# Expert gate and up projections: high and low rows side by side in one 512-column matmul

## The chip, the cores and the metric

The kernel runs on one core of one Trainium2 chip. The metric is the device time of one execution in microseconds (us). TensorE (PE in the profile) multiplies, and its weight loads have a row of their own (PEld). VectorE (DVE), ScalarE (ACT) and GpSimd (POOL) work element by element; SyncE's queue (SP) and POOL's issue transfers. Each engine takes its instructions in the order in which they stand in its queue.

## The reference, cut to what matters

One layer of a diffusion backbone: a token mixer, then a mixture of 16 experts, with float32 throughout. The change lies in the experts. Each expert picks 256 of 2048 tokens, and computes with D = 1024 and EXPERT_FF = 1024

```python
xe = jax.vmap(lambda hb, ib: hb[ib])(h, idx)
hid = jax.nn.silu(jnp.einsum("becd,edf->becf", xe, w_gate)) * jnp.einsum("becd,edf->becf", xe, w_up)
ye = jnp.einsum("becf,efd->becd", hid, w_down) * gate[..., None].astype(h.dtype)
```

and the rows of `ye` are added back at the picked tokens. A final RMSNorm closes the layer.

## The kernel before, in words

Everything up to the routing scores (the mixer) takes the first 1321 us and is not touched. `moe` (from line 1206) then runs the 16 experts one after another.

Float32 products are made of three matmuls of a rounded type: each operand is split into a high part and the low remainder, and `mm3` (line 193) issues high x high (line 194), high x low (195) and low x high (196) into the same PSUM sum. Weights are split by `load_w` (line 167): per half of a 512-column chunk one transfer into `raw` (two buffers), one ACT copy that rounds to `wh` (line 183), one DVE subtraction that gives `wl` (line 184). An expert has six chunks: two of gate, two of up, two of down. Three chunk buffers (two in the pool `wr`, one in `wx`) go round, so a chunk's `wh` can be written only when PE is done with an older chunk.

`expert_in` (line 1364) finds the tokens of the next expert on DVE and PE (`route`, tiles `oh`, `c`, `idx`), gathers their rows with two indirect transfers on POOL's queue (`xg`, line 1368), transposes them on PE (`xt`, line 1376) and splits them into `xS[0]` (high, ACT, line 1378) and `xS[1]` (low, DVE, line 1379), one buffer each. It is called in the middle of the expert before.

`expert` (line 1382) goes over two halves `i` and four blocks `f` of 128 hidden columns. For each it fills one PSUM tile `pg` (name `gu`, 128 x 2 x 256, a whole bank; three buffers): gate in the first 256 columns, up in the other 256, each from 8 steps `k` of `mm3`, 24 matmuls with 256 moving columns. Then ACT takes the SiLU of the gate half out of PSUM (`sgl`, line 1396), DVE multiplies by the up half out of PSUM (1397), ACT rounds the product to `hS[0]` (1399) and DVE makes the remainder `hS[1]` (1400). The down projection (`down`, PSUM name `dn`, two banks) uses 512 moving columns. Results leave by an indirect transfer (1453). In experts 13 and 14 the final norm of all tokens runs beside the matmuls; the last three experts write their rows directly.

The order of each queue is made when the program is built: a scheduler lays the instructions out by its own estimate of their times (`schedule_with_timeline_sim`, line 1567), single matmuls included, so work of neighbouring steps is interleaved. On the chip the queues then run strictly in that order.

Of the kernel before, what the change touches and what calls it, by code (L numbers as in the profile page):

```python
# [7 lines left out]
F32 = mybir.dt.float32  # L8
F32R = mybir.dt.float32r
# [3 lines left out]
AF = mybir.ActivationFunctionType  # L13
OP = mybir.AluOpType
AX = mybir.AxisListType
# [3 lines left out]
P = 128  # L19
D = 1024  # L20
KT = 8
# [1184 lines left out]
def moe(tc, ctx, env):  # L1206
    nc = tc.nc
# [5 lines left out]
    with ExitStack() as pd:  # L1213
# [5 lines left out]
        ps_a = pd.enter_context(tc.tile_pool(name="psaD", bufs=3, space=PS))  # L1219
# [5 lines left out]
        wk = tk.enter_context(tc.tile_pool(name="wkT", bufs=1))  # L1225
# [106 lines left out]
        wk = pd.enter_context(tc.tile_pool(name="wkD", bufs=1))  # L1332

        def route(e):
            oh = ohp.tile([P, 2, 8, 256], BF, name="oh", bufs=1)
            for s in range(2):
                for g in range(8):
                    nc.vector.tensor_scalar(oh[:, s, g, :], siob, SL[:, s, e, g:g + 1], None, op0=OP.is_equal)
            rp = ps_c.tile([P, 2, 256], F32, name="c")
            for hf in range(2):  # L1340
                for i in range(16):
                    s, g = divmod(i, 8)
                    nc.tensor.matmul(rp[:, hf, 0:5], oh[:, s, g, hf * P:(hf + 1) * P], vals[:, s, e, g, :],
                                     start=(i == 0), stop=(i == 15))
            idx = rt.tile([P, 2], I32, name="idx", bufs=2)
            with nc.allow_low_precision(reason="token numbers are whole"):
                nc.vector.tensor_reduce(idx, rp[:, :, 0:2], axis=AX.X, op=OP.add)
            rs = rt.tile([P, 2, 5], F32, name="rs", bufs=2)
            nc.vector.tensor_copy(rs, rp[:, :, 0:5])
            gate = rt.tile([P, 2], F32, name="gate", bufs=2)  # L1350
            nc.vector.tensor_tensor(gate, rs[:, :, 2], rs[:, :, 3], op=OP.add)
            nc.vector.tensor_tensor(gate, gate, rs[:, :, 4], op=OP.add)
            return idx, gate
# [3 lines left out]
        def next_w(src):  # L1357
            if pre:
                return pre.pop(0)
            pool = wx if nchunk[0] % 3 == 2 else wr  # L1360
            nchunk[0] += 1
            return load_w(raw_p, pool, src)

        def expert_in(e):
            idx, gate = route(e)
            xg = wk.tile([P, 2, D], F32, name="xg", bufs=1)
            for hf in range(2):
                last[1] = nc.gpsimd.indirect_dma_start(out=xg[:, hf, :], out_offset=None, in_=f_rows,
                                                       in_offset=bass.IndirectOffsetOnAxis(ap=idx[:, hf:hf + 1], axis=0))
            xS = [wk.tile([P, KT, 256], F32R, name=f"xS{s}", bufs=1) for s in range(2)]  # L1370
            for kk in range(4):
                ps = ps_t.tile([P, 2, 256], F32, name="xt")
                for k2 in range(2):
                    for hf in range(2):
                        k = 2 * kk + k2
                        nc.tensor.transpose(ps[:, k2, hf * P:(hf + 1) * P], xg[:, hf, k * P:(k + 1) * P], ident)  # L1376
                ks = slice(2 * kk, 2 * kk + 2)
                nc.scalar.activation(xS[0][:, ks, :], ps, AF.Copy)
                last[0] = nc.vector.tensor_tensor(xS[1][:, ks, :], ps, xS[0][:, ks, :].bitcast(F32), op=OP.subtract)
            return idx, gate, xS  # L1380

        def expert(e, st, mid=None):
            idx, gate, xS = st
            nx = None
            hS = [wk.tile([P, KT, 256], F32R, name=f"hS{s}", bufs=1) for s in range(2)]
            for i in range(2):
                gw = next_w(w_gate[0, e, :, i * 512:(i + 1) * 512])
                uw = next_w(w_up[0, e, :, i * 512:(i + 1) * 512])
                for f in range(4):
                    fs = slice(f * P, (f + 1) * P)  # L1390
                    pg = ps_a.tile([P, 2, 256], F32, name="gu")
                    for j, w in enumerate((gw, uw)):
                        for k in range(KT):
                            mm3(pg[:, j, :], w[0][:, k, fs], w[1][:, k, fs], xS[0][:, k, :], xS[1][:, k, :], k, KT)
                    sg_ = wk.tile([P, 256], F32, name="sgl", bufs=2)
                    nc.scalar.activation(sg_, pg[:, 0, :], AF.Silu)
                    nc.vector.tensor_tensor(sg_, sg_, pg[:, 1, :], op=OP.mult)  # L1397
                    ff = 4 * i + f
                    nc.scalar.activation(hS[0][:, ff, :], sg_, AF.Copy)  # L1399
                    nc.vector.tensor_tensor(hS[1][:, ff, :], sg_, hS[0][:, ff, :].bitcast(F32), op=OP.subtract)  # L1400
                if mid is not None and i == 0:
                    nx = mid()
# [79 lines left out]

        last = [None, None]
        st = expert_in(0)
        with tc.issue_after(last[1].ins):
            pre.append(load_w(raw_p, wx, w_gate[0, 0, :, 512:1024], cast=C2))
        for e in range(NE):
            nx = mid = None
            if e + 1 < NE:
                if e in MIDE:  # L1490
                    mid = lambda: expert_in(e + 1)
                else:
                    nx = expert_in(e + 1)
            for t in FTS.get(e, ()):
                final_tile(t)
            st = expert(e, st, mid) or nx
# [98 lines left out]
```

## Time and profile before

| | us |
|---|---|
| three runs, median (lowest to highest) | 2491.65 (2488.15 to 2493.32) |
| the profiled execution, its own time | 2490.03 |
| its span, first to last instruction | 2488.2 |
| busy: PE / PEld / DVE / ACT / POOL | 2358.8 / 2156.8 / 1584.1 / 1115.6 / 533.7 |
| stretch of the experts' matmuls | 1321 to 2479 |

How to read it: busy time is a sum over the whole span, and the rows that matter are those of the stretch of the experts. Matmuls are pipelined, so the mean duration of one (some 286 ns) is longer than the distance from the start of one to the start of the next; the distance is what a stream of them costs. "Idle before" is the time for which the engine stood still just before the instruction, with the instruction that released it behind the arrow. The notation 128x2 <- 128x4 is partitions by elements of output and input.

### The profile page before, as it was taken

The page shows a single profiled execution, that of the slowest core. Times are in us where ns is not written, and L with a number is a line of the kernel's source. Part 1 is how long each engine was busy: PE and PEld are TensorE (multiplying, and loading weights), DVE is VectorE, ACT ScalarE, POOL GpSimd, SP SyncE. Part 2 cuts the span into 40 slices and gives each one's busy share as a digit, 9 for nine tenths or more (in the row PEclk, how much of TensorE's full clock was granted, in tenths as well). Part 3 has the DMA queues.
Part 4 walks back from the last instruction along what each step waited for, and adds up shares of the span by engine and source line. Part 5 has one row for each costly group of instructions (what it writes and reads, how often), then busy time and mean ns, then how long its engine had stood idle before and what let it go on. Part 6 is the DMA issues. An engine that isn't in the chain of part 4 may idle for free.

```text
span 2488.2 us, 43191 instructions
## 1 busy us (share of the span) xinstructions
PE 2358.8 (95%) x16841; PEld 2156.8 (87%) x16841; DVE 1584.1 (64%) x3339; ACT 1115.6 (45%) x2004; POOL 533.7 (21%) x451
## 2 busy tenths in 40 slices
PE   7999999999997989999949999999999999999998
PEld 4999999887776888888838899999999999998897
DVE  7588765458778646576774556555565565556675
ACT  4554555567633443333332444444444444444453
POOL 2321222211114553232250101101111011011111
PEclk9999999999998999999978999999999999999999
DMA  8676655489956897655563667666676666668884
GB/s 267 199 229 208 208 172 164 134 269 325 284 142 192 253 278 233 197 187 175 174 189 111 203 187 223 199 205 204 203 220 200 207 219 199 210 203 261 305 301 166
DMA packets 473056, 528.97 MB, mean 213 GB/s; under 512 B 104500, under 2 KB 392061, under 8 KB 470803
## 3 DMA queue, kind: packets, MB, share of 16 engines
q1 hardware_dynamic: 455298, 465.63, 58.6%
q0 software_dynamic: 17120, 59.77, 8.3%
q8 instruction: 133, 2.18, 0.4%
q10 hardware_dynamic: 432, 0.79, 0.1%
q14 instruction: 73, 0.59, 0.1%
HBM read 400.45 MB, written 125.67 MB: 211 GB/s over the span
## 4 chain that ended last, share of the span: by engine, by line
PE 45%; DMA 9%; DVE 3%; issue 3%; ACT 1%; POOL 1%; SPq 0%; POOLq 0%; DVEq 0%; ACTq 0%
PE gu L196 7%; PE gu L194 7%; PE gu L195 7%; PE dn L194 4%; PE dn L195 4%; PE dn L196 4%; DMA xg<-f_rows,idx 4%; PE mx L194 2%; PE mx L196 2%; PE mx L195 2%; DMA raw<-in_w_gate_dram 1%; ACT wh L183 1%; PE xt L1376 1%; DVE wl L184 1%; DMA raw<-in_w_up_dram 1%
## 5 line engine op out<-in xcount | busy, mean ns | idle before, releaser
L184 DVE TENSOR_TENSOR wl<-raw,wh 128x2048 fp32r<-128x2048 f32 (+1 forms) x214 | 450.4, 2116 | 294.2 <-ACT wh L183 291.4
L194 PE MATMUL gu<-xS,wh 128*128 128x256 f32 x2048 | 582.8, 286 | 6.6 <-ACT wh L183 4.7
L196 PE MATMUL gu<-xS,wl 128*128 128x256 f32 x2048 | 580.4, 286 | 4.2 <-DVE wl L184 4.2
L195 PE MATMUL gu<-xS,wh 128*128 128x256 f32 x2048 | 582.0, 285 | 0.0
L183 ACT ACTIVATE wh<-raw 128x2048 fp32r<-128x2048 f32 (+1 forms) x218 | 381.8, 1771 | 356.0 <-DMA raw<-in_w_gate_dram 142.7
L194 PEld LDWEIGHTS gu<-xS,wh 128*128 128x128 f32 x2048 | 395.9, 194 | 8.7 <-ACT wh L183 5.3
L196 PEld LDWEIGHTS gu<-xS,wl 128*128 128x128 f32 x2048 | 394.2, 193 | 6.0 <-DVE wl L184 5.0
L195 PEld LDWEIGHTS gu<-xS,wh 128*128 128x128 f32 x2048 | 396.1, 193 | 1.1
L194 PE MATMUL pj<-aS,wh 128*128 128x258 f32 x832 | 238.7, 290 | 3.1 <-DVE y L460 2.7
L195 PE MATMUL pj<-aS,wh 128*128 128x258 f32 x832 | 239.0, 288 | 0.2 <-DVE aS L358 0.2
L196 PE MATMUL pj<-aS,wl 128*128 128x258 f32 x832 | 238.3, 288 | 0.9 <-DVE wl L184 0.9
L1453 POOL DMA_INDIRECT h_rows<-ye,idx x26 | 67.4, 2591 | 659.8 <-DVE ye L1416 565.7
L194 PE MATMUL dn<-wh,hS 128*128 128x512 f32 (+1 forms) x520 | 202.7, 390 | 0.0
L195 PE MATMUL dn<-wl,hS 128*128 128x512 f32 (+1 forms) x520 | 201.2, 387 | 0.0
L196 PE MATMUL dn<-wh,hS 128*128 128x512 f32 (+1 forms) x520 | 200.3, 386 | 0.0
L194 PEld LDWEIGHTS pj<-aS,wh 128*128 128x128 f32 x832 | 157.7, 191 | 4.7 <-issue 2.4
L195 PEld LDWEIGHTS pj<-aS,wh 128*128 128x128 f32 x832 | 159.2, 191 | 0.6 <-DVE aS L358 0.4
L196 PEld LDWEIGHTS pj<-aS,wl 128*128 128x128 f32 x832 | 158.5, 191 | 1.3 <-DVE wl L184 1.1
L194 PE MATMUL uv<-wh,ast 128*128 128x512 f32 x384 | 153.1, 399 | 0.0
L196 PE MATMUL uv<-wh,ast 128*128 128x512 f32 x384 | 150.2, 391 | 0.0
L195 PE MATMUL uv<-wl,ast 128*128 128x512 f32 x384 | 149.8, 390 | 0.0
L1399 ACT ACTIVATE hS<-sgl 128x256 fp32r<-128x256 f32 x128 | 53.1, 415 | 181.9 <-DVE sgl L1397 181.6
(480 smaller groups left out, 4562.7 us busy)
## 6 DMA issues: line engine op xcount, KB each, us to landing
raw<-in_w_gate_dram SPq DMA_DIRECT2D x64, 1024.0 KB
raw<-in_w_up_dram SPq DMA_DIRECT2D x64, 1024.0 KB
raw<-in_w_down_dram SPq DMA_DIRECT2D x64, 1024.0 KB
kv<-kv SPq DMA_DIRECT2D x140, 256.0 KB
raw<-in_w_mod_dram SPq DMA_DIRECT2D x18, 1024.0 KB
a_sp<-aS SPq DMA_DIRECT2D x32, 512.0 KB
ast<-a_sp POOLq DMA_DIRECT2D x16, 1024.0 KB, 8.6
raw<-in_w_in_dram SPq DMA_DIRECT2D x12, 1024.0 KB
```

Source lines behind the costliest of these rows:

```text
L183: nc.scalar.activation(wh[:, ks, s:s + 256], raw[:, ks], AF.Copy)
L184: (lo_eng or nc.vector).tensor_tensor(wl[:, ks, s:s + 256], raw[:, ks], wh[:, ks, s:s + 256].bitcast(F32), op=OP.subtract)
L194: pace(nc.tensor.matmul(ps, ah, bh, start=(k == 0), stop=False), after)
L195: nc.tensor.matmul(ps, ah, bl, start=False, stop=False)
L196: return nc.tensor.matmul(ps, al, bh, start=False, stop=(k == nk - 1))
L1376: nc.tensor.transpose(ps[:, k2, hf * P:(hf + 1) * P], xg[:, hf, k * P:(k + 1) * P], ident)
L1399: nc.scalar.activation(hS[0][:, ff, :], sg_, AF.Copy)
L1453: nc.gpsimd.indirect_dma_start(out=h_rows, out_offset=bass.IndirectOffsetOnAxis(ap=idx[:, hf:hf + 1], axis=0), in_=ye[:, hf, :], in_offset ...
```

## The change

`xS` becomes one tile with the high rows in its first half and the low rows in its second, `[128, 2, 8, 256]`. In each step `k` the matmuls high x high and high x low, which share the weights `wh`, become one matmul with 512 moving columns (two runs of 256), whose output fills a PSUM bank: high x high in columns 0 to 255, high x low in 256 to 511. Low x high stays a matmul of 256 columns and is added onto the first half. Gate and up so need a bank each, out of the same three buffers. A new VectorE instruction, `tensor_reduce`, sums the two halves of a bank into a float32 tile `gus` in SBUF (two buffers); it reads the bank with a stride of 256 elements, two elements for each of 256 outputs. SiLU and the product then read SBUF in place of PSUM.

```diff
-            xS = [wk.tile([P, KT, 256], F32R, name=f"xS{s}", bufs=1) for s in range(2)]
+            xS = wk.tile([P, 2, KT, 256], F32R, name="xS", bufs=1)
...
-                nc.scalar.activation(xS[0][:, ks, :], ps, AF.Copy)
-                last[0] = nc.vector.tensor_tensor(xS[1][:, ks, :], ps, xS[0][:, ks, :].bitcast(F32), op=OP.subtract)
+                nc.scalar.activation(xS[:, 0, ks, :], ps, AF.Copy)
+                last[0] = nc.vector.tensor_tensor(xS[:, 1, ks, :], ps, xS[:, 0, ks, :].bitcast(F32), op=OP.subtract)
...
-                    pg = ps_a.tile([P, 2, 256], F32, name="gu")
+                    gu_ = wk.tile([P, 2, 256], F32, name="gus", bufs=2)
+                    sg_ = gu_[:, 0, :]
                     for j, w in enumerate((gw, uw)):
+                        pg = ps_a.tile([P, 2, 256], F32, name="gu")
                         for k in range(KT):
-                            mm3(pg[:, j, :], w[0][:, k, fs], w[1][:, k, fs], xS[0][:, k, :], xS[1][:, k, :], k, KT)
-                    sg_ = wk.tile([P, 256], F32, name="sgl", bufs=2)
-                    nc.scalar.activation(sg_, pg[:, 0, :], AF.Silu)
-                    nc.vector.tensor_tensor(sg_, sg_, pg[:, 1, :], op=OP.mult)
+                            nc.tensor.matmul(pg, w[0][:, k, fs], xS[:, :, k, :], start=(k == 0), stop=False)
+                            nc.tensor.matmul(pg[:, 0], w[1][:, k, fs], xS[:, 0, k, :], start=False, stop=(k == KT - 1))
+                        nc.vector.tensor_reduce(gu_[:, j], pg.rearrange("p a f -> p f a"), axis=AX.X, op=OP.add)
+                        if j == 0:
+                            nc.scalar.activation(sg_, sg_, AF.Silu)
+                    nc.vector.tensor_tensor(sg_, sg_, gu_[:, 1, :], op=OP.mult)
```

## Rows read from the trace of the kernel before

**Rows 1.** The page's first part: busy us, share of the span, instructions.

```profile
PE 2358.8 (95%) x16841; PEld 2156.8 (87%) x16841; DVE 1584.1 (64%) x3339; ACT 1115.6 (45%) x2004; POOL 533.7 (21%) x451
```

**Rows 2.** Busy time by stretch: columns first, then the experts and one steady expert's two phases.

```profile
core 0: us, PE busy (x) PEld busy (x) DVE busy (x) ACT busy (x) POOL busy (x), PEclk, DMA share, GB/s
1321.00:2479.00 1158.00, 1141.08 (x8401) 1073.39 (x8398) 685.61 (x896) 500.31 (x556) 151.07 (x92) 0.99 0.68 214
...
1614.30:1660.80 46.50, 46.22 (x403) 45.97 (x402) 24.14 (x42) 19.19 (x22) 6.17 (x4) 1.00 0.69 205
1660.80:1685.40 24.60, 24.60 (x128) 20.71 (x127) 17.95 (x15) 11.24 (x11) 1.62 (x1) 1.00 0.64 212
```

**Rows 3.** What PE waited for between 1321 and 2480 us: total, times, longest.

```profile
PE xt L1376 <- DMA xg<-f_rows,idx: 6.0, 9, 1.1
PE gu L194 <- ACT wh L183: 4.7, 2, 3.2
PE gu L196 <- DVE wl L184: 4.2, 4, 1.5
PE gu L194 <- DVE sgl L1397: 1.9, 1, 1.9
```

**Rows 4.** Matmuls of gate and up in order of time: start, duration; first and last of 24.

```profile
1499.92 0.28 PE L196 MATMUL gu<-xS,wl 128*128 128x256 f32 x1
...
1502.68 0.28 PE L195 MATMUL gu<-xS,wh 128*128 128x256 f32 x1
```

**Rows 5.** Matmuls of the down projection in order of time; first and last of 14.

```profile
1591.72 0.39 PE L194 MATMUL dn<-wh,hS 128*128 128x512 f32 x1
...
1594.67 0.39 PE L195 MATMUL dn<-wl,hS 128*128 128x512 f32 x1
```

**Rows 6.** Groups by line and shape, 1300 to 2488 us: busy, mean ns, idle before and releasers.

```profile
L194 PE MATMUL gu<-xS,wh 128*128 128x256 f32 x2048 | 582.8, 286 | 6.6 <-ACT wh L183 4.7 <-DVE sgl L1397 1.9
L195 PE MATMUL gu<-xS,wh 128*128 128x256 f32 x2048 | 582.0, 285 | 0.0
...
L194 PE MATMUL dn<-wh,hS 128*128 128x512 f32 x504 | 198.2, 393 | 0.0
...
L1400 DVE TENSOR_TENSOR hS<-sgl,hS 128x256 fp32r<-128x256 f32 x128 | 54.3, 424 | 49.3 <-ACT hS L1399 48.9 <-issue 0.5
...
L1397 DVE TENSOR_TENSOR sgl<-sgl,gu 128x256 f32<-128x256 f32 x128 | 53.2, 416 | 82.9 <-ACT sgl L1396 82.7
L1399 ACT ACTIVATE hS<-sgl 128x256 fp32r<-128x256 f32 x128 | 53.1, 415 | 181.9 <-DVE sgl L1397 181.6
L1396 ACT ACTIVATE sgl<-gu 128x256 f32<-128x256 f32 x128 | 47.9, 374 | 91.3 <-PE gu L196 91.3
...
L1379 DVE TENSOR_TENSOR xS<-xt,xS 128x512 fp32r<-128x512 f32 x64 | 42.3, 683 | 1.4 <-ACT xS L1378 1.4
```

**Rows 7.** Groups of DVE before 1321 us: a full-size reduction, a strided copy, a small reduction.

```profile
L478 DVE TENSOR_REDUCE s<-kn 128x4 f32<-128x512 f32 x34 | 22.5, 681 | 8.0 <-ACT kn L476 7.4
...
L766 DVE COPY Tt<-U 96x1024 f32<-96x1024 f32 x6 | 6.5, 1082 | 0.0
...
L653 DVE TENSOR_REDUCE sr<-sq 128x16 f32<-128x128 f32 x1 | 0.3, 284 | 0.0
```

**Rows 8.** What DVE waited for between 1321 and 2480 us: its two longest lines.

```profile
DVE wl L184 <- ACT wh L183: 281.9, 129, 4.3
DVE sgl L1397 <- ACT sgl L1396: 82.7, 36, 6.5
```

**Rows 9.** DVE in order of time across the middle of one expert (idle before in brackets).

```profile
1562.89 2.29 DVE L184 TENSOR_TENSOR wl<-raw,wh 128x2048 fp32r<-128x2048 f32 x1 [2.90 <-ACT wh L183]
1565.10 0.15 DVE L1347 TENSOR_REDUCE idx<-c 128x2 int32<-128x4 f32 x1
```

**Rows 10.** ACT and PE in order of time in the same expert: weight rounding, route, transposes.

```profile
1560.94 3.71 ACT L183 ACTIVATE wh<-raw 128x2048 fp32r<-128x2048 f32 x2 [1.41 <-PE gu L195]
...
1563.74 0.73 PE L1343 MATMUL c<-vals,oh 128*128 128x5 bf16 x23
...
1574.02 0.38 PE L1376 MATMUL xt<-ident,xg 128*128 128x128 f32 x2
1576.83 0.87 PE L1376 MATMUL xt<-ident,xg 128*128 128x128 f32 x6 [1.12 <-DMA xg<-f_rows,idx]
```

**Rows 11.** Busy time by stretch: gate and up of experts 13 and 14 (columns as in group 2).

```profile
2254.20:2306.60 52.40, 48.32 (x404) 47.45 (x404) 28.24 (x49) 20.84 (x29) 10.48 (x9) 0.97 0.87 285
...
2335.00:2386.60 51.60, 47.32 (x381) 46.58 (x380) 30.98 (x38) 24.89 (x34) 15.36 (x13) 0.93 0.90 314
```

## The prediction, made before the changed kernel was run

> **What bounds the kernel now.** I read the page's busy times first: PE is busy for 95% of the span, DVE for 64%, ACT for 45% [rows 1]. A share over the whole span says little, so the next view is the busy time by stretch: between 1321 and 2479 us, where the experts run, PE is busy for 1141 of 1158 us, and in a steady expert for 46.2 of 46.5 us of gate and up and all 24.6 us of down, while DVE works 24.1 and 18.0 us [rows 2]. Third, PE's own waits: 16.8 us in 16 experts, of which 6.0 for the gathered rows, 8.9 for weights, 1.9 for a PSUM tile to be read out [rows 3]. So the experts run at the pace of PE's stream of matmuls, and what an edit of that stream saves arrives at the end, unless another engine takes over as the pacemaker.
>
> **The price of a matmul.** In order of time, 23 steps of gate and up lie between 1499.92 and 1502.68 us: 120.0 ns from start to start with 256 columns [rows 4]. In the down projection 13 steps lie between 1591.72 and 1594.67: 226.9 ns with 512 columns [rows 5]. Doubling the columns adds 106.9 ns, so each matmul carries 120.0 - 106.9 = 13.1 ns that don't depend on its columns. Both kinds load new weights for each matmul, as the changed stream will.
>
> **Part 1, the matmuls.** A step k costs 3 x 120.0 = 360.0 ns now and 226.9 + 120.0 = 346.9 ns after: the columns stay, one matmul in three goes. There are 2048 steps (16 experts x 2 x 4 x 2 x 8; each line counts x2048 [rows 6]), so PE saves 2048 x 13.1 = 26.8 us, 1.7 us an expert. No row has moving columns in two runs with a gap between; the bounds are the two streams: at best 226.9, at worst the 240.0 of two starts. I take 226.9, because the down projection's matmul has the same count of columns and of weight loads.
> The Trainium skill ("TensorE: Matmul & The Clock Gate", section "Back-to-back issue gap") gives N/2.4 + 2.5 ns for an isolated stream, so by it a step falls from 327.5 to 324.9 ns and the change is worth an estimated 5 us. The rows read 120.0 and 226.9 where that gives 109.2 and 215.8, so the measurement decides; the rule speaks against the change and stands among the rivals, beside the mechanism that would bring it about.
>
> **Part 2, the new reduction.** 256 instructions on DVE, 128x256 out of 128x512. A full-size reduction of contiguous SBUF data takes 681 ns, a contiguous read of a 128x512 PSUM tile by DVE 683 ns, and a strided SBUF copy of 1024 elements 1082 ns, 1.06 ns per element [rows 6, 7]. The two reductions of 512 and 128 elements give (681 - 284)/384 = 1.03 ns per element and 152 ns fixed [rows 7]. I take 690 ns; below 681 no row reaches, and the upper bound is an element part that doubles with the stride, 2 x 529 + 152 = 1210 ns. At 690 it is 177 us, 11.0 us an expert. DVE's 24.1 busy us of the gate-and-up phase become 35.1, in a phase that shrinks from 46.5 to 44.8 us [rows 2]; it fits by the sum of busy time, into what is now mostly waiting for the next `wh` (281.9 us in all) [rows 8].
>
> **Part 3, SiLU and product move to SBUF.** The SiLU takes 374 ns out of PSUM; the ACT copy of the same size out of SBUF takes 415, so it costs ACT up to 128 x 41 ns = 5.2 us; DVE's product goes from 416 to some 424 ns, as the remainder does [rows 6]. ACT is busy 19.2 of 46.5 us [rows 2], and this is hidden there; without that cover it would be 5 us. The chain from PE's last matmul of a block to `hS` gets the reduction but loses the SiLU, which now runs beside the up matmuls: 0.69 - 0.37 = 0.3 us longer, behind a down projection whose matmuls never waited [rows 6]. The `xS` layout costs nothing: same instructions, same single buffer. No transfer is added, and none is moved in SP's or POOL's queue; they follow the DVE instructions that release them.
>
> **Part 4, the new waits.** Two are added. ACT's SiLU waits for DVE, and `wh` copies stand behind it; DVE's reduction waits for PE, and `wl`, `idx` and `oh` stand behind it. Three costs follow.
> First, PSUM. A bank was held for a pair (5.76 us) and two spare banks gave 11.5 us before PE had to stop; now a bank is filled every 8 x 346.9 ns = 2.78 us and the spare is 5.55 us. DVE is deaf while it waits for `wh` and subtracts: 2.90 + 2.29 = 5.19 us in a typical case [rows 9], 4.3 + 2.29 = 6.6 at the longest wait [rows 8]. A reduction that becomes ready just as such a stretch begins is over after 5.19 + 0.69 = 5.88 us, 0.33 too late; 1.7 too late in the longest. There are about two such stretches in an expert, so the bounds are 0 (the scheduler puts the reduction first) and 16 x 2 x 0.35 = 11.2 us; I take half, 5.6, because most reductions become ready while DVE is not in such a stretch.
> Second, the gather. `idx` stands on DVE right behind a `wl` [rows 9]. With one reduction ahead of it the rows come 0.69 us later, and PE arrives at the transposes 0.36 us earlier (from 1563.74 to 1574.02 us it runs 80 matmuls, 27 steps x 13.1 ns) [rows 10]. PE already waits there, 1.12 us in this expert [rows 10], 6.0 us over all [rows 3]. Bounds: 0, if the new order moves the transposes back, and 15 x 1.05 = 15.8 us. I take 0.3 us an expert, 4.5 us, since today's mean wait under the same scheduler is 0.4.
> Third, up's second chunk in mid-expert. Its `wl` ends at 1565.18 us, 4.24 us after PE released the buffer [rows 9, 10]. PE needs it two tiles and the routing after the release, 2 x 2.78 + 0.7 = 6.3 us: 2 us of cover hold one reduction ahead of the subtraction, so I cost it at nothing; a second and third reduction ahead would cost up to 0.7 us an expert.
>
> **Part 5, where the saving cannot arrive.** In experts 13 and 14 gate and up take 52.4 and 51.6 us in place of 46.5, with the transfers at 0.87 and 0.90 of their engines in place of 0.69 [rows 2, 11]. PE waits for weights there, so its 1.7 us each go into longer waits: 3.4 us back.
>
> **The sum.** -26.8 + 3.4 + 5.6 + 4.5 = -13.3 us. The profiled execution took 2490.0 us of its own (span 2488.2), so 2476.7; the median of the three runs lies 1.6 above it, so 2478.3.
>
> **The rivals.**
> *The orders eat it.* Both costs of part 4 come in at their upper ends: -26.8 + 3.4 + 11.2 + 15.8 = +3.6, 2495 us. For it: DVE already waits for others for most of its idle time [rows 8] and runs strictly in order. Against: PE waited only 1.9 us for a PSUM tile so far [rows 3].
> *DVE takes over (the slower side).* If the strided read of PSUM costs 1210 ns, the gate-and-up phase holds 24.1 + 16 x 1.21 = 43.5 us of DVE work, and the two stretches in which DVE waits for a released buffer add 2 x 2.9: 49.3 us against PE's 44.8. Then the phase follows DVE: 16 x 4.5 = 72 us above PE's own 2463, some 2535. It decides from (44.8 - 5.8 - 24.1)/16 = 0.93 us for one reduction. For it: no row has a strided read of PSUM. Against: the strided SBUF copy pays nothing per element [rows 7].
> The Trainium skill ("PSUM — Partial Sum Buffer", section "Specifications (TRN2)") says that PSUM's lines are 8 bytes and that a pattern which is not contiguous slows matmuls significantly; if that holds for VectorE's reads too, this rival comes true. No run here shows it yet.
> *The merged matmul is no cheaper.* If two runs of 256 cost two starts, 240 ns, PE saves nothing, and the costs of part 4 remain: +10.1, 2502 us; any saving between 0 and 13.1 ns per step lies between this and the forecast. The gap formula of the Trainium skill, named above, would give such a value.
>
> **How the numbers follow.** The forecast (2464 to 2486) gets 0.55; the orders 0.26, mostly within 2486 to 2497; DVE as the bound 0.12; the merged matmul without gain 0.07. A measurement of this kernel tells about 0.2%, 5 us, from no change. Faster: 0.55 and 0.04 of the orders, 0.59. Same: 0.17 of the orders and 0.02 of the last, 0.19. Slower: 0.05 of the orders, 0.12 and 0.05, 0.22. The range leaves out DVE as the bound (0.12) and some 0.07 of ends: from the whole PE saving with nothing given back (2490.0 - 26.8 = 2463), to 2503.
>
> **What would show it.** Right: gate and up matmuls of 512 columns some 227 ns from the next start, 4096 in place of 6144; 256 reductions of 0.68 to 0.70 us; steady expert phases of about 45 us; PE's waits for reductions under 12 us in all. Wrong: reductions above 0.9 us with DVE busy nearly through gate and up (DVE takes over); many short PE waits for `gu` banks or for `xg` (the orders); starts 240 ns apart (no gain).

## The result

The changed kernel takes 2516.24 us (median of four runs, 2514.62 to 2523.06), the kernel before on the same chip 2489.9 (2482.1 to 2493.32): 1.0107 times as long, 95% interval 1.008 to 1.0134. The forecast was 2478.3 with a range of 2463 to 2503, so the sign was wrong and the time lies 13 us above the range. The profiled execution is the longest of the four (2523.06 us, span 2521.3); from its first gate matmul to its last down matmul it needs 1183.3 us, the one of before 1157.8.

First the engines and the costliest groups of the profile page of the changed kernel (busy us and share of the span; then, by line, busy us, mean ns of one | idle us before it and its releaser):

```profile
PE 2357.0 (93%) x14793; PEld 2043.9 (81%) x14793; DVE 1736.6 (69%) x3595; ACT 1122.0 (44%) x2004; POOL 510.4 (20%) x451
...
L1396 PE MATMUL gu<-xS,wh 128*128 128x512 f32 x2048 | 739.4, 403 | 11.5 <-DVE gus L1398 10.7
L1397 PE MATMUL gu<-xS,wl 128*128 128x256 f32 x2048 | 579.7, 283 | 3.8 <-DVE wl L184 3.8
L1398 DVE TENSOR_REDUCE gus<-gu 128x256 f32<-128x512 f32 x256 | 174.2, 686 | 81.1 <-PE gu L1397 80.2
```

The edit itself did what was forecast. There are 4096 matmuls of gate and up in place of 6144, and a reduction takes 686 ns. Their pace is in PE's timeline of a steady expert, the 512-column matmul of the first and of the last of twelve steps (start, duration):

```profile
1699.78 0.40 PE L1396 MATMUL gu<-xS,wh 128*128 128x512 f32 x1
...
1703.65 0.40 PE L1396 MATMUL gu<-xS,wh 128*128 128x512 f32 x1
```

Eleven steps lie between 1699.78 and 1703.65 us: 352 ns a step. Over the whole trace, by my own count of the starts, it is 351 in place of 360 [rows 4], worth 2048 x 9 = 18 us. Yet PE's busy share fell. What it waited for from its first gate matmul on, 1328 to 2515 us (total us, times, longest):

```profile
PE xt L1376 <- DMA xg<-f_rows,idx: 18.8, 16, 2.5
PE gu L1396 <- DVE gus L1398: 10.7, 10, 2.9
PE dn L194 <- DVE ye L1420: 7.5, 7, 2.2
PE gu L1397 <- DVE wl L184: 3.8, 5, 1.5
PE c L1343 <- DVE rs L1349: 3.2, 1, 3.2
PE dn L195 <- DVE wl L184: 2.3, 2, 1.8
```

These six add up to 46.3 us where [rows 3] had 16.8, and the gathered rows `xg` stand first, 18.8 against 6.0. Behind PE stands DVE, which has a wait that group 8 does not show. DVE's longest waits in the same stretch:

```profile
DVE wl L184 <- ACT wh L183: 153.2, 102, 6.4
DVE gus L1398 <- PE gu L1397: 80.2, 67, 4.2
DVE idx L1347 <- DMA h_rows<-ye,idx: 45.9, 7, 8.3
```

Seven times, for 45.9/7 = 6.6 us on average, VectorE stands still in front of the small reduction that writes `idx`. In the kernel before this happened once, for 9.0 us:

```profile
DVE idx L1347 <- DMA h_rows<-ye,idx: 9.0, 1, 9.0
```

That one, ahead of the third expert, is still there with 8.3 us; the other six are new. One such case, first on DVE (start, duration, in brackets the idle time before):

```profile
1855.03 0.69 DVE L1398 TENSOR_REDUCE gus<-gu 128x256 f32<-128x512 f32 x1 [0.27 <-PE gu L1397]
1855.82 0.43 DVE L1401 TENSOR_TENSOR gus<-gus 128x256 f32<-128x256 f32 x1
1861.79 0.16 DVE L1347 TENSOR_REDUCE idx<-c 128x2 int32<-128x4 f32 x1 [5.54 <-DMA h_rows<-ye,idx]
1862.55 1.28 DVE L1398 TENSOR_REDUCE gus<-gu 128x256 f32<-128x512 f32 x2
```

then the transfers that POOL issues, and the transposes on PE:

```profile
1844.21 1.62 POOL L1457 DMA_INDIRECT h_rows<-ye,idx  x1 [45.56 <-DVE ye L1420]
1852.40 2.52 POOL L1457 DMA_INDIRECT h_rows<-ye,idx  x1 [6.57 <-DMA h_rows<-ye,idx]
1862.74 1.00 POOL L1368 DMA_INDIRECT xg<-f_rows,idx  x1 [7.82 <-issue]
...
1867.11 0.33 PE L1376 MATMUL xt<-ident,xg 128*128 128x128 f32 x1 [0.74 <-DMA xg<-f_rows,idx]
1869.80 1.52 PE L1376 MATMUL xt<-ident,xg 128*128 128x128 f32 x7 [2.36 <-DMA xg<-f_rows,idx]
```

Read it from the top. `idx` has two buffers. The new one for the next expert lies where the previous expert's lay, and the two scatters of the previous expert's results still read that one; the second is issued only at 1852.40. DVE could go on at 1856.25 (1855.82 + 0.43) and stands until the scatter has landed, 5.54 us. Behind it in the same queue wait two reductions, done together at 1862.55, and the gather on POOL, whose rows PE then waits for, 0.74 and 2.36 us. After that wait PE's granted clock was 0.50 for 3.4 us; that window, and one of the two steady experts from 1696.6 to 1844.9 us (us, busy us of PE, PEld, DVE, ACT, POOL, granted clock, DMA share, GB/s):

```profile
1870.10:1873.50 3.40, 3.40 (x15) 3.01 (x14) 1.98 (x2) 0.42 (x1) 0.00 (x0) 0.50 0.97 324
1696.60:1844.90 148.30, 142.05 (x801) 120.23 (x800) 103.59 (x144) 61.36 (x64) 14.96 (x9) 0.99 0.65 199
```

A steady pair of experts takes 148.3 us with PE idle for 6.2 of them; from one pair's last `ye` to the next such a pair took 142 to 143 before.

Why then, and not before? The scheduler laid the routing of the next expert at another place. From the last `ye` of the previous expert (start 1845.14 us) to the point at which DVE is ready for `idx` it is 11.1 us here; in the expert before this one it is 22.4 (last `ye` at 1773.37, `idx` at 1795.81, no wait), and in the kernel before 22.6 (1828.14, 1850.77, no wait). Every other expert has the early place, and there the scatter is not yet home: in the case above `idx` could start only at 1861.79 us, 16.7 us after the last `ye`.

### The profile page after: what moved, and what is told of

Read it like the earlier page. It is cut to its first block, busy times and chain, and to the rows that moved or that the text cites. A ratio compares the mean times of both kernels' runs of the same rounds, so it can differ in the third digit from the quotient of the medians.

```text
span 2521.3 us, 39547 instructions
## 1 busy us (share of the span) xinstructions
PE 2357.0 (93%) x14793; PEld 2043.9 (81%) x14793; DVE 1736.6 (69%) x3595; ACT 1122.0 (44%) x2004; POOL 510.4 (20%) x451
## 5 line engine op out<-in xcount | busy, mean ns | idle before, releaser
L1396 PE MATMUL gu<-xS,wh 128*128 128x512 f32 x2048 | 739.4, 403 | 11.5 <-DVE gus L1398 10.7
L1396 PEld LDWEIGHTS gu<-xS,wh 128*128 128x128 f32 x2048 | 390.3, 191 | 105.9 <-DVE gus L1398 10.8
L1398 DVE TENSOR_REDUCE gus<-gu 128x256 f32<-128x512 f32 x256 | 174.2, 686 | 81.1 <-PE gu L1397 80.2
L1457 POOL DMA_INDIRECT h_rows<-ye,idx x26 | 57.5, 2211 | 734.6 <-DVE ye L1420 644.6
L1403 ACT ACTIVATE hS<-gus 128x256 fp32r<-128x256 f32 x128 | 53.0, 414 | 219.6 <-DVE gus L1401 219.5
L194 PEld LDWEIGHTS dn<-wh,hS 128*128 128x128 f32 x520 | 97.6, 188 | 29.2 <-DVE ye L1420 9.9
```

What stands on the lines that cost most here:

```text
L194: pace(nc.tensor.matmul(ps, ah, bh, start=(k == 0), stop=False), after)
L1396: nc.tensor.matmul(pg, w[0][:, k, fs], xS[:, :, k, :], start=(k == 0), stop=False)
L1398: nc.vector.tensor_reduce(gu_[:, j], pg.rearrange("p a f -> p f a"), axis=AX.X, op=OP.add)
L1457: nc.gpsimd.indirect_dma_start(out=h_rows, out_offset=bass.IndirectOffsetOnAxis(ap=idx[:, hf:hf + 1], axis=0), in_=ye[:, hf, :], in_offset ...
```

## The experiments

Two theories stood at first: (1) the standstill at `idx` is the loss; (2) the reductions on DVE or the 512-column matmuls themselves are. Ratios are to the kernel before on the same chip, with their 95% interval; us worked out from them take 2490 for 100%. By these intervals a difference of two ratios is uncertain by some 0.3%, 7 us. The scheduler makes the order of the queues anew for each kernel; of those below only e8 keeps the order of the kernel before on PE, ACT and POOL. Where starts on PE are counted, the usual distance is the mean from one start to the next for matmuls of one kind, and a start is late when it comes more than a quarter of that distance after it was due. PE's waits are those from 1310 us on, so a wait ahead of the first gate matmul is among them; by that count the kernel before waits 8.9 us for `xg`, the changed one 21.6.

**A third buffer for `idx`**, in the changed kernel (e1) and in the kernel before (e4):

```diff
-            idx = rt.tile([P, 2], I32, name="idx", bufs=2)
+            idx = rt.tile([P, 2], I32, name="idx", bufs=3)
```

> The changed kernel with three buffers for idx in place of two, so that the index of the next expert no longer has to wait until the scatter of the expert before has read its own. Theory 1 (VectorE stands still at idx until that scatter lands, 45.9 us in 7 experts, and reductions and the gather wait behind it): VectorE's wait at idx falls under 5 us, PE's wait for xg from 21.6 to under 10 us, and the time falls from 2516 to 2490 to 2504. Theory 2 (the 174 us of reductions as such overload VectorE's queue, wherever they stand): the wait at idx goes but PE's waits move elsewhere, 2511 to 2520.

Measured: 2512.92 us, 1.0086 (1.0062 to 1.011). The wait did not go; DVE's and PE's waits, then one case on DVE and POOL:

```profile
DVE idx L1347 <- DMA h_rows<-ye,idx: 56.7, 8, 8.4
...
PE gu L1396 <- DVE gus L1398: 35.1, 12, 4.1
...
1620.68 2.05 POOL L1457 DMA_INDIRECT h_rows<-ye,idx  x1 [7.93 <-DMA h_rows<-ye,idx]
...
1630.12 0.16 DVE L1347 TENSOR_REDUCE idx<-c 128x2 int32<-128x4 f32 x1 [7.66 <-DMA h_rows<-ye,idx]
...
1675.50 1.21 POOL L1368 DMA_INDIRECT xg<-f_rows,idx  x1 [52.77 <-PE dn L195]
```

With the buffer to spare the scheduler hoists the routing by a whole expert: the `idx` written at 1630.12 is used by a gather at 1675.50, and the standstill is back one buffer later. The gather is now early, so PE's loss moved from `xg` to the reductions (35.1 us). The experiment changed the order that it was to leave alone; it neither proves nor refutes theory 1, but it shows that the same standstill can reach PE by another road.

> The kernel before with three buffers for idx. It waits at idx for a scatter once (9.0 us), and PE waits 6.0 us for xg. Both theories: within 6 us of the kernel before, so that what e1 gains is a matter of the changed kernel alone.

Measured: 2480.06 us, 0.9945 (0.9928 to 0.9962). The kernel before gets faster with this, by 14 us where at most 6 were expected; its one 9.0 us wait for the scatter is gone.

**The merged matmuls alone (e2).** SiLU and product read the first half of each bank straight out of PSUM; the high x low half is computed and left out of the sum.

```diff
-                    gu_ = wk.tile([P, 2, 256], F32, name="gus", bufs=2)
-                    sg_ = gu_[:, 0, :]
+                    sg_ = wk.tile([P, 256], F32, name="sgl", bufs=2)
...
-                        nc.vector.tensor_reduce(gu_[:, j], pg.rearrange("p a f -> p f a"), axis=AX.X, op=OP.add)
...
-                            nc.scalar.activation(sg_, sg_, AF.Silu)
+                            nc.scalar.activation(sg_, pg[:, 0, :], AF.Silu)
-                    nc.vector.tensor_tensor(sg_, sg_, gu_[:, 1, :], op=OP.mult)
+                    nc.vector.tensor_tensor(sg_, sg_, pg[:, 0, :], op=OP.mult)
```

> The merged matmuls without the reduction: SiLU and product read the first half of each bank straight from PSUM, and the high x low half is left out of the sum (the output lacks this term). Theories 1 and 2: PE keeps the 10 ns saved per step, 20 us, and without reductions VectorE's queue is as before: 2465 to 2478. Theory 3 (the merged matmul or the faster turn of the PSUM banks brings PE's waits): PE's waits as in the changed kernel, 2495 to 2520.

Measured: 2472.59 us, 0.9923 (0.9903 to 0.9943), so 19 us less than before. Its waits on PE:

```profile
PE gu L1396 <- DVE wl L184: 6.2, 4, 2.2
PE xt L1376 <- DMA xg<-f_rows,idx: 5.1, 5, 1.8
PE gu L1395 <- ACT sgl L1398: 4.9, 3, 2.5
PE gu L1395 <- DVE sgl L1399: 4.4, 2, 3.8
```

The saving of the matmuls arrives at the end in full, within the noise. A bank for each projection out of the same three buffers costs PE 9.3 us of waits for banks (the last two rows; 1.9 in [rows 3]), and the kernel is faster all the same: neither the merged matmul nor the bank turnover by itself is what makes the changed kernel slow. `idx` stands where it stood in the kernel before. The one standstill of before is here too, 9.7 us by the profile's view of DVE's waits, which puts it down to `issue`; so "e2 never waited at idx" in the expectation of e10 below misses this one.

**The reductions alone (e3).** Three matmuls of 256 columns as before, high x low into the second half, then the reduction.

```diff
-                            nc.tensor.matmul(pg, w[0][:, k, fs], xS[:, :, k, :], start=(k == 0), stop=False)
+                            nc.tensor.matmul(pg[:, 0], w[0][:, k, fs], xS[:, 0, k, :], start=(k == 0), stop=False)
+                            nc.tensor.matmul(pg[:, 1], w[0][:, k, fs], xS[:, 1, k, :], start=False, stop=False)
```

> The reduction without the merging: three matmuls of 256 columns per step as before, high x low in the second half of the bank, everything else as in the changed kernel. Theory 2: the costs of the changed kernel without its PE saving of 20 us, 2530 to 2545. Theory 1: the same only if the order again puts idx ahead of the scatter; with little wait at idx 2495 to 2515.

Measured: 2548.32 us, 1.0234 (1.02 to 1.0268). The standstill is longer than in the changed kernel:

```profile
DVE idx L1347 <- DMA h_rows<-ye,idx: 74.2, 12, 7.0
...
PE xt L1376 <- DMA xg<-f_rows,idx: 40.4, 28, 3.6
```

The time is 3 us above the range of theory 2; theory 1 allowed it too, if `idx` stood ahead of the scatter again, as it does 12 times here. So this run does not choose between the two. The reductions bring the new order with them; the merged matmuls alone (e2) did not. What a reduction costs in itself and what the order costs had still to be parted.

**The changed kernel with `idx` held back (e5).** The order is told to put the `idx` reduction behind the latest reduction of the current expert that stands in the program ahead of the routing; nothing else is asked for.

```diff
-                        nc.vector.tensor_reduce(gu_[:, j], ...)
+                        mids[0] = nc.vector.tensor_reduce(gu_[:, j], ...)
...
+                if mids[0] is not None:
+                    at.enter_context(tc.issue_after(mids[0].ins))
```

> The changed kernel with the idx reduction of the next expert held, on VectorE's queue, behind the last reduction of the first half of the current expert, where the kernel before had it; two idx buffers as in the changed kernel. With three buffers (e1) the wait at idx stayed (56.7 us), so the buffer count was no clean test. Theory 1 (the standstill at idx behind the scatter is the cause): the wait at idx falls under 5 us, PE's waits for xg and for reductions together from 32 to under 15 us, and the time is 0.5% or more under the changed kernel, 2490 to 2503 where the kernel before takes 2490. Theory 2 (174 us of reductions overload VectorE's queue wherever idx stands): the wait at idx goes, but the time stays at 1.008 to 1.014 of the kernel before.

Measured: 2496.83 us, 1.0021 (1.0005 to 1.0038). That is 0.86% or 21 us less than the changed kernel, as theory 1 had it, and the wait for the scatter is gone from DVE's list. Holding `idx` also moves the gather and what follows it: PE reaches the first transpose of the next expert's rows after 0.73 of an expert's gate and up matmuls (0.71 in the kernel before), in the changed kernel after 0.50 and 0.69 by turns. So 21 us are the price of that order, of which the standstill is the part that the waits show. PE's waits, then DVE's longest:

```profile
PE xt L1380 <- DMA xg<-f_rows,idx: 12.6, 15, 2.1
PE dn L194 <- DVE ye L1424: 8.4, 14, 1.5
PE gu L1401 <- DVE wl L184: 8.0, 4, 3.3
...
PE gu L1400 <- DVE gus L1402: 2.3, 3, 1.2
...
DVE gus L1402 <- PE gu L1401: 127.9, 128, 3.6
DVE wl L184 <- ACT wh L183: 117.8, 90, 2.9
```

Without the standstill the reductions still take back the saving of the matmuls: from e2 to e5 it is 1.0021 - 0.9923 = 0.98%, 24 us. Hardly any of it arrives as waits for a PSUM bank (2.3 us); PE now waits for the gather (12.6 us, 5.1 in e2) and for the down projection's banks to be read out (`ye`, 8.4 us, no such wait before or in e2): work that stands in DVE's queue or behind it comes later.

**The same pair without the merge (e9), and the merge with the order held (e10).** e9 is e3, e10 is e2, each with `idx` held as in e5 (in e10 behind the product).

> e3 (three matmuls, with the reduction) with idx held behind the last reduction of the current expert's first half, as in e5. e3 waited 74.2 us at idx for scatters and took 1.023 of the kernel before. Theory 1 (that standstill is a cause of its own): the wait goes and with it 1.0% or so, as from the changed kernel (1.011) to e5 (1.002): 1.010 to 1.016. If holding idx helped e5 only by reshuffling the order, 1.020 to 1.027.

Measured: 2507.95 us, 1.005 (1.0028 to 1.0071). That is faster than theory 1 had it. The order was worth 2.34 - 0.50 = 1.84% in e3, 46 us.

> e2 (merged matmuls, no reduction; the high x low half is left out of the sum) with idx held as in e5, behind the product of the current expert's first half. e2 never waited at idx. Theory 1: holding idx brings nothing here, 0.990 to 0.995 of the kernel before, and the distance from here to e5 (1.002) is the price of the reductions in a good order. If holding idx is good by itself: under 0.988.

Measured: 2478.53 us, 0.9952 (0.9933 to 0.9972). Here holding `idx` does no good: the gather is late without a reduction in play (PE's waits):

```profile
PE xt L1380 <- DMA xg<-f_rows,idx: 12.1, 8, 1.7
PE gu L1399 <- ACT sgl L1402: 8.7, 3, 3.3
```

Against the kernel before with `idx` held (e12, below, also 0.9952) e10 gains nothing: in the profiled executions, which lie 9.3 us (e10) and 4.5 us (e12) above the medians, the waits of these two rows are 20.8 us where e12 has 3.1, and so as large as the 18 us of the matmuls. So what the merge is worth depends on the order: 0.77% in e2's, nothing that can be measured in e10's. The reductions, added to a kernel with `idx` held, cost 1.005 - 0.9952 = 0.98% without the merge (e9 less e12) and 1.0021 - 0.9952 = 0.69% with it (e5 less e10): 24 and 17 us, which the noise does not tell apart.

**Less work on DVE in the same place (e6).** e5 with a copy of the first half in place of the reduction; high x low is left out.

```diff
-                        mids[0] = nc.vector.tensor_reduce(gu_[:, j], pg.rearrange("p a f -> p f a"), axis=AX.X, op=OP.add)
+                        mids[0] = nc.vector.tensor_copy(gu_[:, j], pg[:, 0])
```

> As e5, with the reduction replaced by a copy of the first half of the bank into the same tile: same waits and same chain, some 0.42 in place of 0.68 us each, 67 us less work on VectorE; the high x low half is left out of the sum. Theory 2, by dose: of the 46 us between merged matmuls alone (0.992 of the kernel before) and the changed kernel (1.011) some 40% go, 0.997 to 1.005 of the kernel before. Theory 1 (waits and order, not the amount of work): within 4 us of e5.

Measured: 2479.52 us, 0.9954 (0.9935 to 0.9974), 0.67% or 17 us less than e5, and below the ranges of both theories. By the groups and PE's waits:

```profile
L1402 DVE COPY gus<-gu 128x256 f32<-128x256 f32 x256 | 106.3, 419 | 71.7 <-PE gu L1401 70.5
...
PE gu L1400 <- DVE gus L1402: 8.7, 6, 2.9
PE xt L1380 <- DMA xg<-f_rows,idx: 6.1, 8, 1.9
```

Dependencies and banks are as in e5, 256 x (686 - 419) ns = 68 us of DVE's work are gone, and a quarter of that comes back at the end. PE's wait for the gather halves and the one for `ye` falls from 8.4 to 0.4 us; the one for banks grows from 2.3 to 8.7. But the order is not that of e5 either: PE reaches the transposes after 0.69 of the gate and up matmuls, in e5 after 0.73. So the run supports, without excluding the order as a rival, that DVE's work is a cost of its own here, though DVE was busy for 64% of the span [rows 1].

**A fourth bank (e7).** e5 with four buffers for `gu` in place of three and one for the transposes in place of two.

```diff
-        ps_a = pd.enter_context(tc.tile_pool(name="psaD", bufs=3, space=PS))
+        ps_a = pd.enter_context(tc.tile_pool(name="psaD", bufs=4, space=PS))
...
-        ps_t = pd.enter_context(tc.tile_pool(name="pstD", bufs=2, space=PS))
+        ps_t = pd.enter_context(tc.tile_pool(name="pstD", bufs=1, space=PS))
```

> As e5, with four PSUM buffers for gate and up in place of three, and one in place of two for the transposes. A tile may then stay unread for 8.3 in place of 5.6 us before PE stops. Theory 4 (the headroom in PSUM is what makes VectorE's lateness cost time): PE's wait for reductions goes to under 3 us and the time falls 8 us or more below e5. Theory 2 (VectorE's lateness reaches PE by every path: gather, remainders, weights): within 5 us of e5.

Measured: 2508.09 us, 1.0068 (1.0047 to 1.009), so slower than e5, which neither theory had. PE waits longer for the reductions, in a kernel with more banks for them:

```profile
PE gu L1400 <- DVE gus L1402: 23.3, 14, 4.4
```

The order changed again, and the transposes lost a bank, so this parts no cost cleanly. It gives no support to the idea that spare banks were the shortage.

**The sum shared between ACT and DVE (e11).** e5, but ACT copies the second half into `gus` and DVE adds the first half out of PSUM.

```diff
-                        mids[0] = nc.vector.tensor_reduce(gu_[:, j], pg.rearrange("p a f -> p f a"), axis=AX.X, op=OP.add)
+                        nc.scalar.activation(gu_[:, j], pg[:, 1], AF.Copy)
+                        mids[0] = nc.vector.tensor_tensor(gu_[:, j], pg[:, 0], gu_[:, j], op=OP.add)
```

> As e5, with the sum made in two steps: ScalarE copies the high x low half to SBUF (0.37 us), and VectorE adds the other half from PSUM, 0.42 in place of 0.68 us each; the sum is complete. If VectorE's 67 us are what separates e5 (1.002) from e6 (0.995), then 0.994 to 0.999 of the kernel before; if ScalarE's 95 us more and the longer chain (two engines and one more wait per bank) cost as much, 1.000 to 1.008.

Measured: 2506.28 us, 1.0059 (1.0038 to 1.008). DVE's part is as short as the copy of e6, and the kernel is slower than with one reduction:

```profile
L1403 DVE TENSOR_TENSOR gus<-gu,gus 128x256 f32<-128x256 f32 x256 | 104.7, 419 | 99.6 <-ACT gus L1402 99.0
...
PE gu L1400 <- DVE gus L1403: 22.7, 19, 2.1
```

DVE now stands for 99 us in front of the add because ACT is not there yet, so what its queue saves in work it can lose by waiting. ACT has 256 copies more to do as well, and this run does not part the two.

**The kernel before, with a tile moved (e8) and with `idx` held (e12).** e4 had shown 0.55% and also other distances between matmuls. e8 adds only an unused 128x2 tile with one memset ahead of `idx`; e12 holds `idx` behind the product.

```diff
+        pad = rt.tile([P, 2], I32, name="pad", bufs=1)
+        nc.vector.memset(pad, 0)
```

> The kernel before with one unused small tile ahead of idx, which moves the tiles behind it in SBUF as the third idx buffer of e4 did; e4 took 0.9945 of the kernel before, with starts of gate and up some 117 in place of 120 ns apart and of down 233 in place of 227. If the place of the tiles sets those distances, this kernel shows them too and takes 0.992 to 0.998; if the third buffer did it through the order, the distances are 120 and 227 and the time is within 0.3% of the kernel before.

Measured: 2488.38 us, 0.9993 (0.9978 to 1.0009). The distances did change (last section); the time did not. By PE's starts the matmuls at their usual distances take 10 us less than in the kernel before; in the profiled execution, the longest of the ten, late starts cost 13 us more.

> The kernel before with idx held behind the product of the current expert's first half. It waits at idx for a scatter once only, 9.0 us. Theory 1: the gain is at most that one wait, 0.994 to 1.001 of the kernel before, so that what holding idx gives to the changed kernel (0.9%) is the repair of the changed kernel's own order. If holding idx helps every version alike: 0.988 to 0.993.

Measured: 2482.39 us, 0.9952 (0.9931 to 0.9972), and PE waits for the gather are down to

```profile
PE xt L1380 <- DMA xg<-f_rows,idx: 3.1, 2, 1.8
```

So the gain of e4 is one of order, not of placement: e4 is 0.48% below e8, with the same distances, and e12 0.48% below the kernel before, with the distances of before. The order without the single 9.0 us standstill is worth about 0.5%, 12 us. How much of that is the standstill itself is open, since in e12 PE also reaches the transposes later (after 0.79 of the gate and up matmuls, 0.71 before). e4 and e12 compute the full result and are faster than both kernels; I found no version with the merged matmuls and their reduction that is.

## Why the prediction was wrong, by its own steps

The measured +1.07% can be reached by two roads. By e2: merging alone -0.77%, the reductions without the standstill +0.98% (e5 less e2), the standstill at `idx` +0.86% (the changed kernel less e5); in us -19, +24, +21. With `idx` held from the start: holding it -0.48% (e12), merging 0.00% (e10), the reductions +0.69% (e5), no longer holding it +0.86%. Each road closes because each part is taken from the one before, so the parts are prices in an order, not constants, and each is uncertain by some 7 us. On both, the reductions cost 17 to 24 us and the order with the standstill 21, and the merge, worth 19 at most, cannot pay for the two.

- **Part 1, the matmuls: right in kind, too large.** -26.8 us became about -18 by the starts and -19 by e2. By the mean of the starts a 512-column matmul with two runs takes 234 ns to the next start here, not 226.9, and the 256-column one after it 117, not 120: 351 a step where 346.9 was forecast. And in the held order (e10) it did not arrive at all. In e1, where the tiles lie elsewhere, it is 229 and 118, 347. No run shows a cost of the two runs as such (contiguous 512 columns stand at 227 to 233 ns in the down projection), and *the merged matmul is no cheaper* falls. The step of 324.9 ns in this part should read 325.0; nothing hangs on it.
- **Part 2, the duration: right; what it costs: the failed step.** 686 ns against 690, and *DVE takes over*, which needed 0.93 us, falls by its own condition. The sentence that failed is "it fits by the sum of busy time, into what is now mostly waiting for the next `wh`". DVE did give up its waiting: 281.9 us [rows 8] became 153.2, and 117.8 in e5. But with that waiting DVE could answer at once when a gather, a `ye` or a `wl` was due: by PE's starts e5 differs from e2 in late starts alone, which cost 58 us against 34, and those at `ye` and at the gather grew by 20. The forecast had 5.6 + 4.5 = 10.1 us for all of this; the runs show 17 to 24, and e6 gives back 17 with 68 us less of DVE's work.
- **Part 3, SiLU and product: right.** The SiLU out of SBUF takes 409 ns (415 at most was forecast), the product 422 (424).
- **Part 4, the waits: two looked at, the third missed.** The bank turnover was put at 5.6 us, within 0 to 11.2; PE's waits for reductions came to 10.7 in the changed kernel, 2.3 in e5, so that bound held. The gather was put at 4.5, at most 15.8; its wait rose by 12.8 (18.8 - 6.0), inside the bound. `ye` is in no term, because the down projection never waited; PE's wait for it came to 7.5 us. The step listed `idx` as something queued behind others. It did not ask what `idx` itself waits for: its buffer, read by a scatter of the expert before. That wait was in the trace of before, once, among DVE's waits, and it stops the whole queue. The order that multiplies it costs 21 us here, 46 in the kernel with the reductions alone.
- **"None is moved in SP's or POOL's queue": true of those queues, and of no help.** Up to expert 13 both queues issue in the order of before. But, as the sentence goes on, the gather follows the instruction that releases it, and that one was moved by the scheduler in DVE's queue: 11.1 us after the last `ye` in every other expert, in place of 22.6. The prediction took the order of before for the order of after, though the section on the kernel says that a scheduler makes it from its own estimates.
- **The rival *the orders eat it* was the right mechanism with too small an upper end.** It stopped at 2495 because it added the bounds of two waits; a standstill of the queue and the later arrival of everything else on DVE were not in it. Nor was it the forecast: 0.26 against 0.55.
- **Part 5** forecast that the PE saving of experts 13 and 14 is given back (3.4 us). From the last matmul of one down projection to the first of the next their gate and up take 47.6 us each (in expert 13 with 16 of 256 matmuls still to come), against 52.6 and 51.9 before ([rows 11], by the same count): here the forecast was on the wrong side, and no run parts what shifted. In e2 (50.0 and 53.5) and e5 (52.3 and 51.2) nearly nothing was gained there, as forecast.
- **Where the 25.5 us of the stretch lie.** The waits of the six rows are 29.5 us longer than those of [rows 3] and the matmuls 18 shorter, so 14 us stand in no wait row: idle time is counted from the modelled end of a matmul (a duration of 403 ns at 234 from start to start), which hides short gaps. PE's starts close the sum. With every start at its usual distance the stretch would take 1121 us before and 1102 after, 19 less; late starts cost 37 us before and 82 after, 45 more. Of the 82, 22 lie at the gathered rows (7 before), 12 at banks that wait for a reduction, 9 at `ye`, and 27 (17 before) where the profile shows no idle time.
- **What stays open.** No run has the reductions in the order that the matmuls have without them. So how much of the 17 to 24 us is DVE's work and how much the order made for it is argued from the waits and from e6, not shown.

## What to carry to other kernels

When an edit adds work to an in-order queue, don't set it against the idle share of that engine: ask for each kind of instruction in the queue who waits for it, and count the added work as delay of all of them. For each instruction in that queue that reuses a buffer, look who reads the old contents, above all a transfer that lands late; one row of that kind in the trace of before, even with a total of 9 us, is a stall that any new order can multiply. Where the order is made anew by a scheduler, give the new order a range of its own: here it moved the end by 21 us in one kernel and 46 in another while the reductions took the time that was forecast.

## What the runs showed of the hardware that was not expected

**The pace of matmuls follows where tiles lie in SBUF.** e8 leaves the order of all instructions on PE, ACT and POOL as it was and only shifts tiles. Gate and up, first and last of 20, and the down projection, first and last of 15:

```profile
1499.80 0.28 PE L196 MATMUL gu<-xS,wl 128*128 128x256 f32 x1
...
1502.01 0.28 PE L194 MATMUL gu<-xS,wh 128*128 128x256 f32 x1
...
1599.69 0.40 PE L195 MATMUL dn<-wl,hS 128*128 128x512 f32 x1
...
1602.95 0.40 PE L194 MATMUL dn<-wh,hS 128*128 128x512 f32 x1
```

That is 2.21/19 = 116 ns and 3.26/14 = 233 ns, where [rows 4, 5] have 120.0 and 226.9. The forecast subtracted those two numbers to get the fixed part of a matmul (13.1 ns); in e8 the same subtraction, 2 x 116.3 - 232.9, gives nothing (-0.3 ns). By the same count e4, whose tiles are moved too, has 117 and 233, and e12, whose tiles lie as before, 120 and 228. So 13.1 was no constant of the engine, and a term of 13.1 x 2048 rested on a difference that moves by as much with a tile's place. Which tile and which property of its place does it was not tried.

**VectorE read PSUM with a stride at no extra cost.** Two elements 1024 bytes apart for each output took 686 ns, the contiguous reduction in SBUF 681 [rows 7].
The Trainium skill ("PSUM — Partial Sum Buffer", section "Specifications (TRN2)") says of patterns that are not contiguous that they slow matmuls; it was weighed as a rival for VectorE's reads, and the 686 ns do not agree with carrying it over to them.

**After some waits PE's clock fell.** After standing for 0.74 and 2.36 us at the transposes, PE worked from 1870.10 to 1873.50 us at a granted clock of 0.50, which is 1.2 GHz, the lower level. In PE's timeline there two steps of gate and up start 1.28 us apart, 640 ns a step in place of 351:

```profile
1871.76 0.63 PE L1396 MATMUL gu<-xS,wh 128*128 128x512 f32 x1
...
1873.04 0.61 PE L1396 MATMUL gu<-xS,wh 128*128 128x512 f32 x1
```

By my count of starts that lie twice as far apart, the changed kernel has eight such stretches in the experts' part, and the four between 1500 and 2200 us each follow two waits at the transposes, 0.5 to 1.0 and 2.0 to 2.5 us; the kernel before has four, and none between 1420 and 2280 us. A wait of that length is not always followed by it: after one of 2.19 us in front of a down matmul at 1833.93 us the granted clock from 1834 to 1840 us is 1.00. Starts twice as far apart cost 11 to 12 us in either kernel, so the clock is no part of the 25.5 us.
